# Softmax sums of an attention kernel: all key-tile additions on VectorE, first copies on GpSimd

## The chip, the cores and the metric

The kernel runs on one core of a Trainium2 chip. A core has a matrix engine (TensorE, shown as PE; its weight loads as PEld), a vector engine (VectorE, DVE), an activation engine (ScalarE, ACT), a general engine (GpSimd, POOL) and a sync engine (SyncE, SP) that here issues nearly all DMAs. They run side by side, each working through its own instructions in a fixed order, and meet at semaphores. The metric is the device time of one execution in microseconds; the median of the runs counts.

## What is computed

Two layers of a backbone over 256 context and 1,024 latent tokens, all in float32. Each layer has an input projection, four mixers side by side (a convolution, a gated linear attention called gla, a softmax attention, and a retention called ret), an output projection and an MLP. The part that matters is the softmax attention: 4 query heads share 2 key heads, 64 wide.

```python
def gqa_attend(q, k, v):
    s = jnp.einsum('bkgqd,bksd->bkgqs', q, k, preferred_element_type=jnp.float32) * ATT_DH ** -0.5
    p = jax.nn.softmax(s, axis=-1).astype(v.dtype)
    return jnp.einsum('bkgqs,bksd->bkgqd', p, v)
```

In layer 0 context and latent tokens are queries; in layer 1 only latent tokens are. Latent queries see all 1,280 keys, context queries only the 256 context keys.

## The kernel before

Tokens are cut into three tiles, t = 0 (256 context tokens), 1 and 2 (512 latent tokens each). Keys are taken 128 at a time: 10 key tiles for a latent token tile, 2 for the context tile.

`attention(g, side)` serves one key head g and its two query heads h_ = 0 and 1. It returns three generators: `prep` loads and transposes q and k, `rowmaxes` finds each query's largest score (matmuls into the PSUM tiles mb and pb, a maximum on VectorE, L972, and a few very small operations, L976 to L979), and `main(t)` does the softmax itself with keys on the partitions and queries along the columns. Its loop over key tiles, L1001 to L1022, is a pipeline one step deep. In step s, for each head: two matmuls write the scores of key tile s into an sb bank (L1006, L1007; two banks in all), and ScalarE takes the exponential into an SBUF tile aP (L1009; each head has its own aP with two buffers). For key tile s-1, for each head: a matmul of the values with aP adds to the output bank ob (L1014; the trace shows two PE instructions for each, since the data is float32), and the exponentials are added element by element to a running sum `sm[h_]`, a 128x512 tile that the trace calls acc (L1015 to L1021). The first key tile is copied into the sum instead (L1019). After the loop, matmuls with ones sum over the partitions (L1025), ScalarE forms the reciprocal with Ln and Exp (tile arc, L1027 and L1028), and VectorE multiplies into the result y (L1029).

Who does the copy and the additions is chosen by head: head 0 goes to GpSimd, head 1 to VectorE.

```python
eng = (nc.gpsimd, nc.vector)[h_]
if j == 0:
    eng.tensor_copy(sm[h_][:, :n], p_[:, :n])
else:
    eng.tensor_tensor(sm[h_][:, :n], sm[h_][:, :n], p_[:, :n], op=ALU.add)
```

An aP buffer can be written again when both its matmul and its addition are done, two steps later.

Attention is interleaved with the other mixers: `attend()` is stepped inside two loops, `pass1` (gla1 and ret1) and `pass2` (gla2 and ret2), and then drained. pass2 has GpSimd work of its own: L841 and L916 build the tiles gqe and rqe for small matmuls. After the drain the output projection loads its weights (wst), splits each into a rounded part on ScalarE (L159, whi) and a rest on VectorE (L160, wlo), splits y in the same way (ahi, alo), and starts the matmuls into `bank`.

The order in which each engine gets its instructions isn't the order of the code. A scheduler in the compiler orders them by their data, the free buffers, their place in the code and modelled durations, over all engines at once. So the weight splits of the output projection are found among the last steps of attention, and the two heads of a key tile do not always follow each other. A matmul helper `mm` has L166, a transpose helper `tr` L163, the activation helper `act` L153, so these lines appear for many stages; the tiles tell them apart.

Of the kernel before, what the change touches and what calls it, by code (L numbers as in the profile page):

```python
# [12 lines left out]
ALU = mybir.AluOpType  # L13
# [80 lines left out]
def build(tc, a, out, dbg=None):  # L94
    cst = a["cst"]
    nc = tc.nc
# [14 lines left out]
    def bank(tag="bank"):  # L111
        pool, bufs = P[tag]
        return pool.tile([128, 512], F32, tag=tag, name=tag, bufs=bufs)
# [104 lines left out]
    def open_w(slabs=5, stages=3):  # L218
        W["p"] = pools.get("wp", side="right", bufs=slabs)
        W["st"] = stages  # L220
# [136 lines left out]
            nc.vector.scalar_tensor_tensor(lo[:, k, :], s[:, :n], sh, hi[:, k, :].bitcast(F32),  # L357
                                           op0=ALU.add, op1=ALU.subtract)

    # ------------------------------------------------------------------ start  # L360
    open_w()
    open_act()
    xt = [xy_tile(t, "x") for t in range(3)]
# [50 lines left out]
    for l in range(2):  # L414
        last = l == 1
        tts = [1, 2] if last else [0, 1, 2]

        # -------------------------------------------------------- in projections
        def colA(sl, c0, t):
            b = bank()  # L420
            n = TOK[t][1]
            hi, lo = h[t]
            mm3(b[:, :n], [(sl[k // 2][0][:, k % 2, c0:c0 + 128], sl[k // 2][1][:, k % 2, c0:c0 + 128], hi[:, k, :], lo[:, k, :])
                           for k in range(KD)])
            return b
# [64 lines left out]
        for t in tts:  # L490
            o, n = TOK[t]
# [15 lines left out]
        for t in tts:  # L507
            o, n = TOK[t]
# [7 lines left out]

        pools.close("sg")

        # attention operands: rms norm and rotation, token-major
        aa = pools.get("aa", bufs=2)  # L520
        cosa = aa.tile([128, 8, 32], F32, name="cosa", bufs=1)
        sina = aa.tile([128, 8, 32], F32, name="sina", bufs=1)
# [64 lines left out]
        if l == 0:  # L587
            drain(small)

        # gated linear attention operands: decays, decayed queries and keys  # L590
        ag = pools.get("ag", bufs=2)
        tri = ag.tile([128, 512], F32, name="tri", bufs=1)
        ind = ag.tile([128, 2], F32, name="ind", bufs=1)
# [111 lines left out]
            emit_msc(0, 1)  # L705
        pools.close("ar", "convp", "actp", "wp", "psd")

        # -------------------------------------------------------- mixers
        open_psum("psa", sb=2, ob=1, mb=1, pb=1)
        open_psum("psm", gb0=1, gb1=1, rb=1)  # L710

# [218 lines left out]
        pass1 = both(stagger((gla1(i) for i in range(NTILE)), 3), stagger((ret1(i) for i in range(NTILE)), 3))  # L930
        pass2 = both(stagger((gla2(i) for i in back), 4), stagger((ret2(i) for i in back), 4))

        # -------------------------------------------------------- attention, one key head at a time
        at_ = pools.get("at", bufs=2)
        def attention(g, side):
            ap_ = pools.get(f"ap{g}", side=side, bufs=2)
            qa = ap_.tile([128, 2, NT], F32R, name="qa", bufs=1)
            ka = ap_.tile([128, NT], F32R, name="ka", bufs=1)
            kb = ap_.tile([66, NT], F32R, name="kb", bufs=1)
            mneg = ap_.tile([128, NTILE, 2, 2], F32R, name="mneg", bufs=1)  # L940
            ve = ap_.tile([128, NTILE, 64], F32, name="ve", bufs=1)
            nc.scalar.copy(kb[64:66, :], ones[0:2, 0:1].to_broadcast([2, NT]))

            def prep(i):
                need_q = not (last and i < CT)
                h0 = 0 if need_q else 2
                rw = at_.tile([128, 3, 64], F32, tag="arw", name="arw", bufs=4)
                nc.sync.dma_start(out=rw[:, h0:3, :], in_=attraw[i, :, g, h0 * 64:192].rearrange("p (h d) -> p h d", d=64))
                nc.sync.dma_start(out=ve[:, i, :], in_=attraw[i, :, g, 192:256])
                yield  # L950
                b = bank("pb")
                for j in range(h0, 3):
                    tr(b[0:64, j * 128:(j + 1) * 128], rw[:, j, :])
                cs = slice(i * 128, (i + 1) * 128)
                kp = b[0:64, 256:384]
                nc.scalar.copy(ka[0:64, cs], kp)
                nc.scalar.copy(ka[64:128, cs], kp)
                nc.vector.tensor_tensor(kb[0:64, cs], kp, ka[0:64, cs].bitcast(F32), op=ALU.subtract)
                if need_q:
                    qp = b[0:64, 0:256].rearrange("p (a b) -> p a b", a=2)  # L960
                    nc.scalar.copy(qa[0:64, :, cs], qp)
                    nc.vector.tensor_tensor(qa[64:128, :, cs], qp, qa[0:64, :, cs].bitcast(F32), op=ALU.subtract)

            def rowmax(i, h_):
                cs = slice(i * 128, (i + 1) * 128)
                kts = [(0, 256)] if i < CT else [(0, 512), (512, 512), (1024, 256)]
                mx = at_.tile([128, 4], F32, tag="amx", name="amx", bufs=4)
                for j, (ko, kn) in enumerate(kts):
                    b = bank(("mb", "pb")[(h_ + j) % 2])
                    mm(b[:, :kn], qa[:, h_, cs], ka[:, ko:ko + kn], True, False)  # L970
                    mm(b[:, :kn], qa[0:64, h_, cs], kb[0:64, ko:ko + kn], False, True)
                    nc.vector.reduce_max(mx[:, j:j + 1], b[:, :kn], axis=AX.X)  # L972
                    yield
                m = mx[:, 0:1]
                if len(kts) > 1:
                    nc.vector.reduce_max(mx[:, 3:4], mx[:, 0:3], axis=AX.X)  # L976
                    m = mx[:, 3:4]
                nc.vector.tensor_scalar(mneg[:, i, h_, 0:1], m, -1.0, None, op0=ALU.mult)
                nc.vector.scalar_tensor_tensor(mneg[:, i, h_, 1:2], m, -1.0, mneg[:, i, h_, 0:1].bitcast(F32),  # L979
                                               op0=ALU.mult, op1=ALU.subtract)  # L980

            def rowmaxes(t, h_):
                o, n = TOK[t]
                for j in range(n // 128):
                    yield from rowmax(o // 128 + j, h_)

            def main(t):
                o, n = TOK[t]
                qb = [ntmp(F32R) for h_ in range(2)]
                b = bank("sb")  # L990
                for h_ in range(2):
                    nc.scalar.copy(qb[h_][0:64, :n], qa[0:64, h_, o:o + n].bitcast(F32))
                    for j in range(n // 128):
                        mm(b[64 * h_:64 * h_ + 2, j * 128:(j + 1) * 128], mneg[:, o // 128 + j, h_, :].bitcast(F32), ident, True, True)
                    nc.scalar.copy(qb[h_][64:66, :n], b[64 * h_:64 * h_ + 2, :n])
                yield
                kts = list(range(CT if t == 0 else NTILE))
                bo = bank("ob")
                sm = [nacc() for h_ in range(2)]
                ps = {}  # L1000
                for step_ in range(len(kts) + 1):  # L1001
                    if step_ < len(kts):
                        js = slice(step_ * 128, (step_ + 1) * 128)
                        for h_ in range(2):
                            bs = bank("sb")
                            mm(bs[:, :n], ka[:, js], qa[:, h_, o:o + n], True, False)  # L1006
                            mm(bs[:, :n], kb[:, js], qb[h_][0:66, :n], False, True)  # L1007
                            p_ = at_.tile([128, 512], F32, tag=f"aP{h_}", name="aP")
                            act(p_[:, :n], bs[:, :n], AF.Exp, "exp", scale=0.125)  # L1009
                            ps[step_, h_] = p_  # L1010
                    if step_ > 0:
                        j = step_ - 1
                        for h_ in range(2):
                            mm(bo[64 * h_:64 * h_ + 64, :n], ve[:, j, :], ps[j, h_][:, :n], j == 0, j == kts[-1])  # L1014
                        for h_ in range(2):  # L1015
                            p_ = ps.pop((j, h_))
                            eng = (nc.gpsimd, nc.vector)[h_]
                            if j == 0:
                                eng.tensor_copy(sm[h_][:, :n], p_[:, :n])  # L1019
                            else:  # L1020
                                eng.tensor_tensor(sm[h_][:, :n], sm[h_][:, :n], p_[:, :n], op=ALU.add)  # L1021
                    yield  # L1022
                bs = bank("sb")
                for h_ in range(2):
                    mm(bs[64 * h_:64 * h_ + 64, :n], ones[:, 0:64], sm[h_][:, :n], True, True)  # L1025
                rc = at_.tile([128, 512], F32, tag="arc", name="arc", bufs=1)
                act(rc[:, :n], bs[:, :n], AF.Ln, "exp")  # L1027
                act(rc[:, :n], rc[:, :n], AF.Exp, "exp", scale=-1.0)  # L1028
                nc.vector.tensor_tensor(y[t][:, 4 + g, :], bo[:, :n], rc[:, :n], op=ALU.mult)  # L1029

            return prep, rowmaxes, main
# [53 lines left out]
        if "y" in dbg and dbg.get("l", 0) == l:  # L1085
            for t in tts:
                o, n = TOK[t]
                nc.sync.dma_start(out=dbg["y"][:, :, o:o + n], in_=y[t])

        # -------------------------------------------------------- out projection  # L1090
        open_dense()
        open_act()
        w_out = a["w_out"][l].rearrange("(k p) n -> p k n", p=128)
# [2 lines left out]
        for dh in range(2):  # L1096
            sl = [load_slab(w_out[:, 2 * q:2 * q + 2, dh * 512:(dh + 1) * 512], 2, 512) for q in range(4)]
            for t in tts:
                o, n = TOK[t]
# [18 lines left out]
                    h2[t] = act_tile(t)  # L1118
                    norm_mod(l, 1, xt[t], t, h2[t], acc[t])

        # -------------------------------------------------------- mlp
        w_up = a["w_up"][l].rearrange("(k p) n -> p k n", p=128)
        w_dn = a["w_down"][l].rearrange("(f p) n -> p f n", p=128)
        NF = FC // 128
# [83 lines left out]
        if "x" in dbg and dbg.get("l", 0) == l:  # L1208
            for t in tts:
                o, n = TOK[t]  # L1210
# [36 lines left out]
```

## Time and profile before

| what | before |
| --- | --- |
| runs | 3320.23, 3351.21, 3358.03 us |
| median | 3351.21 us |
| span of the profiled execution | 3332.9 us |
| PE, DVE, ACT, POOL busy | 97%, 53%, 28%, 7% of the span |

The span goes from the first to the last instruction of one profiled execution. The page gives no time for that execution beyond its span. The span is 18.3 us below the median of the runs and 12.7 us above the fastest of them. The attention loop with its sums occupies two stretches of it, about 570 to 795 us in layer 0 and 2305 to 2499 us in layer 1. A stage is read from its own stretch: which engine is busy there, who waits for whom, and how long one instruction of a kind takes.

### The profile page before, as it was taken

The page shows a single profiled execution, that of the slowest core. Times are in us where ns is not written, and L with a number is a line of the kernel's source. Part 1 is how long each engine was busy: PE and PEld are TensorE (multiplying, and loading weights), DVE is VectorE, ACT ScalarE, POOL GpSimd, SP SyncE. Part 2 cuts the span into 40 slices and gives each one's busy share as a digit, 9 for nine tenths or more (in the row PEclk, how much of TensorE's full clock was granted, in tenths as well). Part 3 has the DMA queues.
Part 4 walks back from the last instruction along what each step waited for, and adds up shares of the span by engine and source line. Part 5 has one row for each costly group of instructions (what it writes and reads, how often), then busy time and mean ns, then how long its engine had stood idle before and what let it go on. Part 6 is the DMA issues. An engine that isn't in the chain of part 4 may idle for free. (4 is left out here: it accounts for less than half of the span.)

```text
span 3332.9 us, 42190 instructions
## 1 busy us (share of the span) xinstructions
PE 3248.3 (97%) x17209; PEld 2475.9 (74%) x17209; DVE 1762.8 (53%) x3026; ACT 920.1 (28%) x1839; POOL 245.8 (7%) x255
## 2 busy tenths in 40 slices
PE   7999989999999999999999999899999999999999
PEld 5778856556888888888888779666557788888887
DVE  4683344676554444454446892235674644444545
ACT  4123432334322111111113334322243311111222
POOL 0011110331000000000000020201340000000000
PEclk8999997999999999999999999858899999999999
DMA  8354131003122222211111222210003111111111
GB/s 277 94 161 133 62 109 35 14 17 117 37 91 83 89 83 76 89 51 39 39 38 59 87 82 79 73 60 29 4 29 120 57 40 43 51 51 51 51 38 51
DMA packets 206523, 232.26 MB, mean 70 GB/s; under 512 B 19714, under 2 KB 160728, under 8 KB 206328
## 3 DMA queue, kind: packets, MB, share of 16 engines
q1 hardware_dynamic: 205592, 227.84, 21.4%
q8 instruction: 135, 2.21, 0.3%
q0 software_dynamic: 736, 1.72, 0.2%
q14 instruction: 60, 0.49, 0.0%
HBM read 191.11 MB, written 38.40 MB: 69 GB/s over the span
## 5 line engine op out<-in xcount | busy, mean ns | idle before, releaser
L166 PE MATMUL bank<-ahi,whi 128*128 128x512 f32 (+1 forms) x1920 | 720.0, 375 | 13.5 <-ACT tmp L153 6.6
L166 PE MATMUL bank<-ahi,wlo 128*128 128x512 f32 (+1 forms) x1920 | 720.5, 375 | 0.0
L166 PE MATMUL bank<-alo,whi 128*128 128x512 f32 (+1 forms) x1920 | 719.6, 375 | 0.9 <-DVE alo L357 0.9
L1156 DVE SCALAR_TENSOR_TENSOR x<-bank,mods,x 128x512 f32<-128x512 f32 (+1 forms) x640 | 438.5, 694 | 260.7 <-PE bank L166 259.0
L166 PE MATMUL bank<-hh,whi 128*128 128x512 f32 (+1 forms) x1280 | 475.9, 372 | 0.0
L166 PE MATMUL bank<-hl,whi 128*128 128x512 f32 (+1 forms) x1280 | 475.3, 371 | 0.0
L166 PE MATMUL bank<-hh,wlo 128*128 128x512 f32 (+1 forms) x1280 | 473.9, 370 | 0.0
L166 PEld LDWEIGHTS bank<-ahi,whi 128*128 128x128 f32 x1920 | 364.8, 190 | 100.5 <-DVE x L1156 8.2
L166 PEld LDWEIGHTS bank<-alo,whi 128*128 128x128 f32 x1920 | 362.9, 189 | 73.3 <-DVE alo L357 2.0
L166 PEld LDWEIGHTS bank<-ahi,wlo 128*128 128x128 f32 x1920 | 362.2, 189 | 67.8 <-issue 2.1
L160 DVE TENSOR_TENSOR wlo<-wst,whi 128x1024 fp32r<-128x1024 f32 (+1 forms) x186 | 224.9, 1223 | 269.1 <-ACT whi L159 268.9
L159 ACT CAST whi<-wst 128x1024 fp32r<-128x1024 f32 (+1 forms) x186 | 191.6, 1044 | 621.6 <-PE bank L166 473.1
L166 PEld LDWEIGHTS bank<-hh,whi 128*128 128x128 f32 x1280 | 240.5, 188 | 45.6
L166 PEld LDWEIGHTS bank<-hh,wlo 128*128 128x128 f32 x1280 | 239.9, 187 | 46.5 <-issue 0.2
L166 PEld LDWEIGHTS bank<-hl,whi 128*128 128x128 f32 x1280 | 240.4, 188 | 43.9 <-issue 0.2
L1140 ACT ACTIVATE tmp<-bank 128x512 f32<-128x512 f32 (+1 forms) x160 | 88.4, 553 | 658.5 <-PE bank L166 657.4
L1142 DVE TENSOR_TENSOR tmp<-tmp 128x512 f32<-128x512 f32 (+1 forms) x160 | 102.0, 639 | 308.5 <-ACT hh L1141 306.7
L166 PE MATMUL bank<-whi,ahi 128*128 128x512 f32 (+3 forms) x640 | 220.1, 346 | 8.3 <-ACT whi L159 8.3
L166 PE MATMUL bank<-wlo,ahi 128*128 128x512 f32 (+3 forms) x640 | 219.9, 344 | 4.2 <-DVE wlo L160 4.2
L166 PE MATMUL bank<-whi,alo 128*128 128x512 f32 (+3 forms) x640 | 216.6, 339 | 0.0
L463 DVE SCALAR_TENSOR_TENSOR yacc<-u,wdw,yacc 128x1295 f32<-128x1295 f32 (+1 forms) x120 | 166.4, 1432 | 0.3
L166 PEld LDWEIGHTS bank<-whi,ahi 128*128 128x128 f32 x640 | 122.0, 191 | 30.1 <-issue 9.2
(240 smaller groups left out, 3731.2 us busy)
## 6 DMA issues: line engine op xcount, KB each, us to landing
wm<-in_w_mod_dram SPq DMA_DIRECT2D x96, 512.0 KB, 4.1
wst<-in_w_up_dram SPq DMA_DIRECT2D x64, 512.0 KB, 4.2
wst<-in_w_down_dram SPq DMA_DIRECT2D x64, 512.0 KB, 3.5
wst<-in_w_in_dram SPq DMA_DIRECT2D x32, 512.0 KB, 4.6
graw<-glaraw SPq DMA_DIRECT2D x18, 512.0 KB, 3.4
wst<-in_w_out_dram SPq DMA_DIRECT2D x16, 512.0 KB, 4.0
x<-xdram SPq DMA_DIRECT2D x4, 2048.0 KB
glaraw<-gpre SPq DMA_DIRECT2D x18, 384.0 KB, 2.3
```

The lines of the kernel that those rows point to most:

```text
L159: nc.scalar.copy(hi, src)
L160: nc.vector.tensor_tensor(lo, src, hi.bitcast(F32), op=ALU.subtract)
L166: nc.tensor.matmul(ps, lhsT=lhsT, rhs=rhs, start=start, stop=stop)
L463: nc.vector.scalar_tensor_tensor(yv, uv, wv, yv, op0=ALU.mult, op1=ALU.add)
L1140: nc.scalar.activation(rl[:, :n], b[:, :n], AF.Relu)
L1142: nc.vector.tensor_tensor(rl[:, :n], rl[:, :n], rl[:, :n], op=ALU.mult)
L1156: nc.vector.scalar_tensor_tensor(xt[t][:, d, :], b[:, :n], mod(l, 5, d, seg), xt[t][:, d, :], op0=ALU.mult, op1=ALU.add)
```

## The change

The choice of the engine goes from the head to the kind of operation. Both heads' first copies are on GpSimd, and both heads' additions on VectorE. Eight comment lines become blank lines; they issue nothing. The core of the diff:

```diff
                         for h_ in range(2):
                             p_ = ps.pop((j, h_))
-                            eng = (nc.gpsimd, nc.vector)[h_]
                             if j == 0:
-                                eng.tensor_copy(sm[h_][:, :n], p_[:, :n])
+                                nc.gpsimd.tensor_copy(sm[h_][:, :n], p_[:, :n])
                             else:
-                                eng.tensor_tensor(sm[h_][:, :n], sm[h_][:, :n], p_[:, :n], op=ALU.add)
+                                nc.vector.tensor_tensor(sm[h_][:, :n], sm[h_][:, :n], p_[:, :n], op=ALU.add)
                     yield
```

## Rows read from the trace of the kernel before

**Rows 1.** The page, whole span: busy time, share and instructions of each engine.

```profile
PE 3248.3 (97%) x17209; PEld 2475.9 (74%) x17209; DVE 1762.8 (53%) x3026; ACT 920.1 (28%) x1839; POOL 245.8 (7%) x255
```

**Rows 2.** Windows of both attention stretches: busy us (instructions) by engine, then clock, DMA.

```profile
core 0: us, PE busy (x) PEld busy (x) DVE busy (x) ACT busy (x) POOL busy (x), PEclk, DMA share, GB/s
570.00:790.00 220.00, 218.01 (x1124) 115.95 (x1125) 149.41 (x353) 85.69 (x199) 73.11 (x60) 0.98 0.09 28
...
2305.00:2495.00 190.00, 190.00 (x926) 98.97 (x923) 129.99 (x294) 69.75 (x158) 67.17 (x56) 0.94 0.03 9
```

**Rows 3.** Waits, 565 to 800 us: engine, line waited for, total us, times, longest.

```profile
ACT aP L153 <- PE sb L166: 72.5, 46, 6.1
...
PEld sb L166 <- DVE acc L1021: 2.6, 2, 2.1
...
PEld sb L166 <- POOL acc L1021: 1.4, 2, 1.0
PE sb L166 <- DVE acc L1021: 1.2, 1, 1.2
```

**Rows 4.** Line L1021: count, ns min/median/max, forms. Then groups of VectorE by form (busy us, mean ns).

```profile
L1021 POOL TENSOR_TENSOR acc<-acc,aP x74: 724/1274/1964, 577.1 to 2496.8; 128x512 f32<-128x512 f32 x72, 128x256 f32<-128x256 f32 x2
L1021 DVE TENSOR_TENSOR acc<-acc,aP x74: 417/1441/1777, 577.4 to 2497.2; 128x512 f32<-128x512 f32 x72, 128x256 f32<-128x256 f32 x2
...
L1021 DVE TENSOR_TENSOR acc<-acc,aP 128x512 f32<-128x512 f32 x72 | 88.6, 1230 | 32.4 <-ACT aP L153 32.1
...
L757 DVE TENSOR_TENSOR fo<-fo,fss 128x256 f32<-128x256 f32 x36 | 19.8, 563 | 3.5 <-ACT fss L153 3.5
...
L1019 DVE COPY acc<-aP 128x512 f32<-128x512 f32 x8 | 3.3, 418 | 0.2 <-ACT aP L153 0.2
L1019 DVE COPY acc<-aP 128x256 f32<-128x256 f32 x2 | 1.1, 552 | 0.0
L1021 DVE TENSOR_TENSOR acc<-acc,aP 128x256 f32<-128x256 f32 x2 | 0.8, 421 | 0.1
```

**Rows 5.** Timeline, layer 0, heads in step: start us, us, engine, line, operation, count, idle before.

```profile
773.69 1.08 PE L166 MATMUL ob<-aP,ve 128*64 128x512 f32 x4
774.13 1.27 POOL L1021 TENSOR_TENSOR acc<-acc,aP 128x512 f32<-128x512 f32 x1 [0.88 <-ACT aP L153]
774.50 1.44 DVE L1021 TENSOR_TENSOR acc<-acc,aP 128x512 f32<-128x512 f32 x1 [0.71 <-ACT aP L153]
...
775.85 1.08 PE L166 MATMUL ob<-aP,ve 128*64 128x512 f32 x4
...
777.69 0.60 ACT L153 ACTIVATE aP<-sb 128x512 f32<-128x512 f32 x1
```

**Rows 6.** Timeline, layer 0, heads one at a time.

```profile
762.36 1.07 PE L166 MATMUL ob<-aP,ve 128*64 128x512 f32 x2
763.23 0.68 DVE L1021 TENSOR_TENSOR acc<-acc,aP 128x512 f32<-128x512 f32 x1
764.02 1.07 PE L166 MATMUL ob<-aP,ve 128*64 128x512 f32 x2
764.93 1.28 POOL L1021 TENSOR_TENSOR acc<-acc,aP 128x512 f32<-128x512 f32 x1 [1.71 <-ACT aP L153]
```

**Rows 7.** Timeline of PE: the first and the last such pair of ob matmuls.

```profile
573.69 1.07 PE L166 MATMUL ob<-aP,ve 128*64 128x512 f32 x2
...
2478.02 1.07 PE L166 MATMUL ob<-aP,ve 128*64 128x512 f32 x2
```

**Rows 8.** Timeline, layer 0, the end of the last 512-column tile.

```profile
782.74 1.58 POOL L1021 TENSOR_TENSOR acc<-acc,aP 128x512 f32<-128x512 f32 x1 [0.64 <-ACT aP L153]
783.10 1.76 DVE L1021 TENSOR_TENSOR acc<-acc,aP 128x512 f32<-128x512 f32 x1
...
784.79 1.21 DVE L160 TENSOR_TENSOR wlo<-wst,whi 128x1024 fp32r<-128x1024 f32 x1
785.92 0.68 DVE L1021 TENSOR_TENSOR acc<-acc,aP 128x512 f32<-128x512 f32 x1
...
786.66 1.07 PE L166 MATMUL sb<-acc,ones 128*64 128x512 f32 x2 [1.22 <-DVE acc L1021]
```

**Rows 9.** Timeline, layer 1, the last additions before the sums.

```profile
2496.82 1.27 POOL L1021 TENSOR_TENSOR acc<-acc,aP 128x512 f32<-128x512 f32 x1 [0.86 <-ACT aP L153]
2497.20 1.44 DVE L1021 TENSOR_TENSOR acc<-acc,aP 128x512 f32<-128x512 f32 x1 [0.69 <-ACT aP L153]
```

**Rows 10.** Windows, as group 2: two stretches of low clock inside attention.

```profile
621.00:634.00 13.00, 13.00 (x59) 8.16 (x57) 3.01 (x5) 1.93 (x4) 1.44 (x2) 0.61 0.01 1
...
2347.00:2372.00 25.00, 25.00 (x63) 11.49 (x62) 6.99 (x15) 5.38 (x10) 2.55 (x2) 0.53 0.00 0
```

**Rows 11.** Timeline of POOL, layer 0: a first copy behind pass2's work.

```profile
707.92 1.04 POOL L841 TENSOR_TENSOR gqe<-gq,c_blk 128x512 f32<-128x512 f32 x1 [6.31 <-PE gb L166]
708.90 0.81 POOL L1019 COPY acc<-aP 128x512 f32<-128x512 f32 x1
```

## Prediction

> **What bounds the kernel now.** I read the page first, then the windows of the two stretches in which the changed lines run, then the waits there, then the timeline of single steps. The page says that PE is busy for 97% of the span and POOL for 7% [rows 1]. That is a mean over stages, so the windows decide: in attention PE is busy 218.0 of 220 us in layer 0 and 190.0 of 190 in layer 1, while DVE is at 149.4 and 130.0, that is 68% each, and POOL at 73.1 and 67.2 [rows 2]. The engine whose work changes is not the one that is full.
>
> The waits say the same from the other side. ScalarE, which writes the exponentials, waits 72.5 us for the score matmuls (PE sb). In the same answer no row has it waiting for an addition to give back an aP buffer. PE itself stood idle once for an addition, for 1.2 us; the weight loads waited 2.6 us for VectorE's additions and 1.4 for GpSimd's [rows 3]. These few waits stand at the ends of tiles, where the matmuls with ones need the finished sums.
>
> A single step shows how much room the additions have. With the heads in step, the ob matmuls of two successive key tiles start at 773.69 and 775.85: a step takes 2.16 us of PE. The additions of one key tile start at 774.13 (POOL) and 774.50 (DVE) and end at 775.40 and 775.94. The buffer that the first of them read is written again at 777.69 [rows 5]. So an addition could come 2.3 us later (777.69 less 775.40), more than a whole step, before ScalarE noticed.
>
> **The price of an addition.** VectorE's 72 additions of 128x512 have a median of 1.44 us and a mean of 1.23 [rows 4], but one that meets no GpSimd addition takes 0.68 us [rows 6]. Where the two meet, VectorE's ends 0.54 us after GpSimd's: 775.94 against 775.40 [rows 5]. So the long ones are spent waiting for GpSimd, and the change takes that neighbour away. I price an addition after the change at 0.68 us (0.42 at 128x256); the upper end is 1.44. GpSimd's copies could hold additions up in the same way: 20 copies at no more than the 0.81 us of the one in [rows 11] are between 0 and 16 us.
>
> The Trainium skill gives a rule for this: "SBUF — State Buffer", section "Who interferes with whom", says that a VectorE instruction with two SBUF inputs and a GpSimd instruction that reads SBUF share a read interface, and that the later one is blocked until the other is done. The trace agrees, with 1.44 us beside GpSimd and 0.68 without. The rule speaks against the new place of the copies, which read SBUF too: by it the sum for VectorE tends to the upper of the two ends just given, and without it to the lower. The time of the kernel is the same by both as long as VectorE isn't full.
>
> **The change part by part.**
>
> *GpSimd loses 74 additions.* At a median of 1.27 us that is some 94 us of POOL [rows 4], off the path. It gains ten copies (two for each token tile and key head), 0.81 us at most by [rows 11]. Nothing shown waits for POOL in these stretches except the sums, so this part is worth nothing by itself.
>
> *VectorE gains 74 additions and loses ten copies.* After: 144 x 0.68 + 4 x 0.42 = 99.6 us. Before: 88.6 + 0.8 for its additions and 3.3 + 1.1 for its copies, 93.8 us [rows 4]. The difference is +5.8 us for twice the additions. Other VectorE work is stretched in the same way by GpSimd: the 36 multiplications of L757 took 563 ns on average, against 421 for an addition of the same width [rows 4], so up to 5.1 us go back. VectorE's load over both stretches, 279 us [rows 2], changes by +0.7 to +5.8 us (+22 with the copies at their worst), and goes from 68% to at most 74%. PE's 100% covers it. Without that cover, were VectorE the bound, this would cost these 0.7 to 22 us.
>
> *In one step.* Head 0's addition would run from 774.13 to 774.81 and head 1's from there to 775.49, before the 775.94 of today [rows 5]. The buffers come free earlier, which nobody waits for.
>
> *The ends of the tiles.* Here something is on the path. At the end of layer 1 the sums wait for the additions that end at 2498.09 and 2498.64 [rows 9]. One after the other on VectorE they would end at 2497.50 and 2498.18: 0.5 us earlier. At the end of layer 0's last wide tile the last addition ends at 786.60, since VectorE has weight splits of 1.21 us in between and an addition was held to 1.76 us; PE stood still for 1.22 us [rows 8]. Head 0's additions, 0.68 us each, take the place of such holds. Depending on where the splits fall, the last one ends about 1.2 us earlier or as late as now; I take 1.2, because the blocked time alone (1.76 less 0.68 for one addition) is nearly that much. The other tile ends are covered by interleaved matmuls.
>
> *New wait.* The addition of key tile 1 of head 1 now waits for a copy on GpSimd. That copy's queue also holds pass2's L841 and L916, and one L841 had waited 6.31 us for PE just before a copy [rows 11]. Behind the waiting addition on VectorE stand the row maxima, and for their banks PE waits. At the start of the ten tiles this is bounded by 0 and 10 x 6.31 = 63 us. I take 0: a copy normally has a whole step before its addition is due.
>
> *The order.* The compiler's scheduler orders all engines by modelled times, so PE's order may come out differently too. This is the largest unknown. PE is fast when the two heads' ob matmuls follow each other (four in 1.08 us) and slow when they come alone (two in 1.07): then half a step lasts 764.02 - 762.36 = 1.66 us, 3.32 for both heads instead of 2.16 [rows 5, 6]. Each half-step alone costs 0.58 us. Fifteen of the 160 wide half-steps are alone; the first and the last stand in [rows 7]. All of them in step would give 8.7 us; all 160 alone would cost 84. I take 0, since the additions have those 2.3 us of room and so need not move PE's order.
>
> **Sum.** 0.5 + 1.2 = 1.7 us less. The profiled span would go from 3332.9 to 3331.2 us. What lies around that span isn't given; the median of the runs is 18.3 us above it, and the runs lie 37.8 us apart. I put the sum on the median: 3351.2 - 1.7 = 3349.5 us. That can't be told from no change: about 1% (33.5 us) is what a measurement of this kernel can tell.
>
> **Rivals.**
>
> *Slower: the heads fall out of step.* Both heads' additions now queue on one engine, head 1's always last, behind row maxima and splits. If its buffer comes free late in the scheduler's model, PE's order alternates between heads. At 0.58 us each, 58 more half-steps alone make it 1% slower; with 80 it is 3396 us, with all 145 it is 3434. For it: this already happens at the start of tiles [rows 6, 7]. Against it: the 2.3 us of room.
>
> *Slower: VectorE waits behind GpSimd's copies,* as above. With three tiles of ten it is 3349.5 + 19 = 3368 us; it decides only from six tiles on.
>
> *An addition takes 1.44 us for itself.* Then two need 2.88 us in a step of 2.16, and VectorE bounds the steps where attention runs nearly alone. The timeline has 13 of them like the one in [rows 5]; at 0.72 us each that is 9.4 us: 3359. Against it: the 0.68 us of [rows 6].
>
> *Faster: order and clock fall well.* Inside attention the granted clock lay at 0.61 for 13 us and at 0.53 for 25 us [rows 10], that is mostly at 1.2 GHz instead of 2.4. If another order avoids both, 13 x 0.39 and 25 x 0.47 us are gone, 16.8 together, and with all heads in step 8.7 more: 3324 us. Nothing in the change aims at it. The same unknown can add a stretch.
>
> *VectorE is the bound in spite of PE's 100%.* The PEld share in the same windows is only 53% and 52% [rows 2]. Then VectorE's +0.7 to +5.8 us show directly: 3350 to 3355. The Trainium skill ("Perfetto Trace Analysis", section "Identifying the Most-Contended Engine") says that matmul busy time is a poor measure of headroom and weight-load busy time a better one. The trace does not bear out that VectorE is the bound: it idles for a third of the time, and PE hardly waits for it [rows 2, 3].
>
> **How the numbers follow.** The forecast, nothing that can be told apart, with VectorE as the bound included: 0.78; its own range is that of the runs, 3320 to 3358 less the 1.7, so 3318 to 3356. Out of step: 0.07. Behind the copies: 0.05. Additions of 1.44: 0.03. Order and clock: 0.07. Past 1%: faster takes half of the last case and 0.05 for the scatter of the runs, 0.09. Slower takes most of the first (0.05), a little of the second (0.02) and 0.05 for scatter, 0.12. Same: 0.79. The range goes from the fastest run less all heads in step, 3320.2 - 8.7 = 3311.5, to the slowest plus as many half-steps again alone and one more stretch of low clock like the longer one, 3358.0 + 8.7 + 11.8 = 3378.5.
>
> **What would show it.** Right: L1021 on DVE x148 with a median near 0.68 us; POOL with 20 copies and no addition; DVE's share near 70% and PE's near 100% in attention; ob matmuls in fours; the sums after layer 0's last wide tile about 1 us after the last exponential's matmul. Wrong: many ob matmuls in twos (out of step); DVE idle before L1021 with POOL as the releaser (behind the copies); L1021 still at 1.44 us; a stretch of low clock that is new or gone.

## The result, and the profile after

The changed kernel takes 3375.25 us (median of 18 runs, 3348.78 to 3398.15), the kernel before 3348.99 (18 runs, 3320.23 to 3377.95). The ratio is 1.0093, with a 95% interval of 1.0067 to 1.0118. (Ratios here compare fast runs alone, those within 1.5% of the fastest of their kernel, so a ratio can differ a little from that of two medians.) The forecast was no difference. The change makes the kernel a little slower: 0.9%, inside the range on record and short of 1%, but clearly apart from nothing.

In the profiled execution the span is 3380.6 us, where it was 3332.9. The page after, which answers to [rows 1], columns as there:

```profile
PE 3297.3 (98%) x17209; PEld 2497.6 (74%) x17209; DVE 1760.1 (52%) x3090; ACT 919.8 (27%) x1839; POOL 155.7 (5%) x191
```

GpSimd is 90 us less busy. VectorE has 64 instructions more and is not busier. In these two executions the time is in PE: 49 us more busy, with the same 17,209 instructions.

The additions themselves (view of the changed line L1020 and of the copies' line L1018, then VectorE's groups by form; they answer to [rows 4]):

```profile
L1020 DVE TENSOR_TENSOR acc<-acc,aP x148: 409/686/839, 606.2 to 2544.9; 128x512 f32<-128x512 f32 x144, 128x256 f32<-128x256 f32 x4
L1018 POOL COPY acc<-aP x20: 397/610/1172, 598.2 to 2521.5; 128x512 f32<-128x512 f32 x16, 128x256 f32<-128x256 f32 x4
...
L1020 DVE TENSOR_TENSOR acc<-acc,aP 128x512 f32<-128x512 f32 x144 | 95.3, 687 | 28.8 <-ACT aP L153 28.6
L757 DVE TENSOR_TENSOR fo<-fo,fss 128x256 f32<-128x256 f32 x36 | 19.0, 556 | 3.1 <-ACT fss L153 3.1
...
L1020 DVE TENSOR_TENSOR acc<-acc,aP 128x256 f32<-128x256 f32 x4 | 2.2, 570 | 0.0
```

An addition over 512 columns now takes 0.687 us on average. Before, VectorE's took 1.23, with a median of 1.44. No long ones are left: the longest takes 0.839. Of the 28.8 us that VectorE idled before these additions, 28.6 ended with ScalarE's exponentials, and none is put down to a copy on GpSimd.

The windows of both attention stretches after (columns as in [rows 2]):

```profile
597.00:822.00 225.00, 224.55 (x1071) 118.36 (x1070) 137.36 (x369) 76.04 (x182) 27.26 (x28) 0.91 0.06 18
2343.00:2543.00 200.00, 198.27 (x932) 99.89 (x932) 129.78 (x327) 70.14 (x161) 25.20 (x25) 0.94 0.03 9
```

PE is as full as before, and VectorE is at 61% and 65%. So the loss doesn't show as a wait: PE has the same matmuls to do and needs longer for them. Two things can do that, the order of the matmuls and the clock. The order first. A half-step is one head's part of a step, wide when it has 512 columns; it is alone when the ob matmuls of the other head don't stand beside its own. Timeline of PE in the changed kernel, layer 1, one piece with the heads one at a time and one with the heads in step:

```profile
2497.82 1.07 PE L166 MATMUL ob<-aP,ve 128*64 128x512 f32 x2
...
2498.82 0.50 PE L166 MATMUL sb<-qa,ka 128*128 128x512 f32 x1
2499.16 0.39 PE L166 MATMUL sb<-tmp,kb 66*128 66x512 f32 x1
2499.48 1.07 PE L166 MATMUL ob<-aP,ve 128*64 128x512 f32 x2
...
2541.85 1.08 PE L166 MATMUL ob<-aP,ve 128*64 128x512 f32 x4
...
2544.01 1.94 PE L166 MATMUL ob<-aP,ve 128*64 128x512 f32 x8
```

Alone, a half-step takes 2499.48 - 2497.82 = 1.66 us; a whole step in fours takes 2544.01 - 2541.85 = 2.16. Both are the values of [rows 5, 6]. The two heads write different halves of the ob bank, and four matmuls of both (1.08 us) take no longer than two of one head (1.07). What has changed is how many there are of each kind. In the program, 38 of the 160 wide half-steps are alone, where the kernel before has 16 (the prediction counted 15 in the trace). PE's order is the same until some way past the first ob matmul of layer 0, and 354 of its 15,029 matmuls and transposes stand at another place, all inside the attention stretches.

The clock. Windows of 150 us around both attentions (the last three columns are granted clock, DMA share, GB/s), first the kernel before:

```profile
450.00:600.00 150.00, 147.71 (x1155) 92.03 (x1155) 73.70 (x193) 42.02 (x144) 16.08 (x15) 0.89 0.19 56
600.00:750.00 150.00, 149.71 (x763) 82.29 (x761) 102.51 (x252) 53.82 (x132) 52.68 (x44) 0.97 0.05 13
2100.00:2250.00 150.00, 137.01 (x832) 91.25 (x830) 45.38 (x126) 37.35 (x114) 15.13 (x20) 0.67 0.23 71
2250.00:2400.00 150.00, 149.99 (x850) 84.76 (x850) 81.31 (x193) 39.94 (x102) 31.14 (x27) 0.86 0.05 17
```

and the changed kernel:

```profile
450.00:600.00 150.00, 148.44 (x952) 91.95 (x952) 56.08 (x152) 33.44 (x121) 8.93 (x10) 0.66 0.16 47
600.00:750.00 150.00, 149.69 (x775) 84.77 (x774) 89.23 (x236) 47.58 (x118) 21.28 (x22) 0.87 0.05 15
2100.00:2250.00 150.00, 135.59 (x858) 100.83 (x857) 49.56 (x124) 55.61 (x139) 19.23 (x25) 0.83 0.26 83
2250.00:2400.00 150.00, 149.99 (x936) 89.94 (x935) 69.08 (x187) 34.28 (x105) 11.00 (x12) 0.80 0.09 28
```

In the first window the changed execution has a clock of 0.66 against 0.89, that is more of the stretch at 1.2 GHz instead of 2.4. The first ob matmul comes at 600.92 us instead of 573.69, although PE's order up to there is the same. So some 27 of the 47.7 us between the two spans arose before any matmul stood at another place. Two single profiles can't show the effect of this change; it needs many runs, with each run's clock beside its time.

### The profile page after: what moved, and what is told of

It is laid out like the page before. It is cut to its first block, busy times and chain, and to the rows that moved or that the text cites. A ratio compares the mean times of both kernels' runs of the same rounds, so it can differ in the third digit from the quotient of the medians.

```text
span 3380.6 us, 42195 instructions
## 1 busy us (share of the span) xinstructions
PE 3297.3 (98%) x17209; PEld 2497.6 (74%) x17209; DVE 1760.1 (52%) x3090; ACT 919.8 (27%) x1839; POOL 155.7 (5%) x191
```

## How the experiments are read

Each run has its time and the mean granted clock of its core over the span. Over all runs that recorded both (235 runs of 14 kernels), one straight line for all kernels, with a level of its own for each kernel, leaves a scatter of 1.8 us. Its slope is 2.9 us for 0.001 of clock. From lowest to highest, the runs of one kernel lie 0.7 to 2.3% apart, almost only through their clock. The levels compare the kernels at the same mean clock, with 95% intervals of 1 to 2 us. The raw ratio stands beside them, because the clock that a kernel gets can be part of what it does.

"Alone" is the number of wide half-steps, of 160, that are left over when neighbouring ob matmuls of the two heads are paired off in the program's order; the groups of ob matmuls in each trace agree with it. One run of e9 at a mean clock of 0.663 (4320.68 us) is left out of the level.

| kernel | alone | ratio to before, 95% | mean clock | level against before, us |
| --- | --- | --- | --- | --- |
| before | 16 | 1 | 0.956 | 0 |
| after | 38 | 1.0093, 1.0067 to 1.0118 | 0.954 | +15.5 ± 0.9 |
| e1 after's engines, before's order | 16 | 1.0027, 0.999 to 1.0064 | 0.954 | +0.2 ± 1.1 |
| e2 before's engines, after's order | 38 | 1.0063, 1.0026 to 1.0101 | 0.954 | +15.6 ± 1.1 |
| e3 after's engines, heads in step | 2 | 1.0003, 0.9966 to 1.004 | 0.955 | -6.3 ± 1.1 |
| e4 before's engines, heads in step | 2 | 0.998, 0.9945 to 1.0016 | 0.956 | -9.9 ± 1.1 |
| e5 additions moved alone | 34 | 1.0049, 1.0016 to 1.0081 | 0.955 | +13.1 ± 1.1 |
| e6 copies moved alone | 14 | 0.9998, 0.9964 to 1.0031 | 0.957 | -0.2 ± 1.1 |
| e7 additions half as wide | 14 | 0.9976, 0.9941 to 1.0011 | 0.957 | -5.0 ± 1.1 |
| e8 before's engines, heads alternate | 136 | 1.024, 1.0199 to 1.0281 | 0.955 | +72.5 ± 1.5 |
| e9 after, third aP buffer | 34 | 0.9944, 0.9913 to 0.9976 | 0.961 | +9.6 ± 1.3 |
| e11 the same again | 34 | 0.9968, 0.993 to 1.0006 | 0.963 | +8.8 ± 1.2 |
| e10 before, maxima twice | 78 | 1.0222, 1.0189 to 1.0255 | 0.948 | +67.7 ± 1.6 |
| e12 e10 with before's order | 16 | 1.022, 1.0163 to 1.0276 | 0.944 | +35.7 ± 1.6 |

The question to them: is it the moved work on the engines, or the order in which TensorE gets its matmuls? And if the order, what moved it?

## Experiments 1 and 2: engines and order apart

In e1 the changed kernel gets TensorE's order from the kernel before, in e2 the kernel before gets the order of the changed one. Matmuls and transposes are noted down as they are issued, and before the program is ordered, each is tied to the one before it in a given list, without a semaphore. The list covers the attention stretches of both layers.

```diff
-        nc.tensor.matmul(ps, lhsT=lhsT, rhs=rhs, start=start, stop=stop)
+        return seen(nc.tensor.matmul(ps, lhsT=lhsT, rhs=rhs, start=start, stop=stop))
...
-    pools.close("psd", "dram", "xy01", "xy2", "nrm", "cpool")
+    force(tc, PEI, PE_ORDER); pools.close("psd", "dram", "xy01", "xy2", "nrm", "cpool")
...
+def force(tc, pei, orders):
+    for seq in orders:
+        for x, y_ in zip(seq, seq[1:]):
+            tc.add_manual_dep(pei[f"I-{y_}"], f"I-{x}", mybir.DependencyInfo(mybir.DependencyClass.NoSync,
+                              mybir.DependencyReason.DATA), reason="order")
```

> The changed kernel (all additions on VectorE, all first copies on GpSimd), but TensorE gets its matmuls of both attention stretches in exactly the order of the kernel before: 16 wide half-steps alone in place of 38. Theory A, the order: the 0.9% is the price of TensorE's order alone, so this is as fast as the kernel before, ratio 1.000 (0.997 to 1.003). Rival B, the engines: VectorE carries twice the additions and holds up TensorE, whatever the order, so the ratio stays at 1.009. Rival C, half and half: 22 half-steps alone at 0.58 us are 12.8 us, 0.4%; the other 0.5% comes from lower clock or from waits and stays, ratio 1.005.

> The kernel before (head 0 on GpSimd, head 1 on VectorE), but TensorE gets its matmuls of both attention stretches in exactly the order of the changed kernel: 38 wide half-steps alone in place of 16. Theory A, the order: as slow as the changed kernel, ratio 1.009. Rival B, the engines: 1.000. Rival C: 1.004, the 12.8 us of the half-steps without what the engines or the clock add.

Measured: e1 3356.12 us, e2 3372.12, beside 3355.86 for the kernel before. At the same clock e1 is at +0.2 us and e2 at +15.6, and the changed kernel is at +15.5. Whoever has the new order has the loss, and whoever has the new engines under the old order has none. By the raw ratios alone the two intervals overlap; it is the level at equal clock that separates them. VectorE's additions by form, first e1, then e2:

```profile
L1020 DVE TENSOR_TENSOR acc<-acc,aP 128x512 f32<-128x512 f32 x144 | 95.3, 687 | 28.5 <-ACT aP L153 25.3 <-ACT fss L153 2.9
```

```profile
L1021 DVE TENSOR_TENSOR acc<-acc,aP 128x512 f32<-128x512 f32 x72 | 86.8, 1205 | 36.8 <-ACT aP L153 36.4
```

e1 has the short additions of the changed kernel without its loss; e2 has the long ones of the kernel before (1205 ns on average) and the loss. PE in e2, with a GpSimd addition between two half-steps alone:

```profile
2485.56 1.07 PE L166 MATMUL ob<-aP,ve 128*64 128x512 f32 x2
2486.47 1.28 POOL L1021 TENSOR_TENSOR acc<-acc,aP 128x512 f32<-128x512 f32 x1 [3.11 <-ACT aP L153]
...
2487.22 1.07 PE L166 MATMUL ob<-aP,ve 128*64 128x512 f32 x2
```

It is the 1.66 us of the changed kernel, with the old engines.

## Experiments 3, 4 and 8: what one half-step alone costs

The same way of holding the order, with other lists: in e3 (engines of the changed kernel) and e4 (of the kernel before) the ob matmuls of both heads stand side by side; in e8, on the engines of the kernel before, head 0's are moved ahead of head 1's score matmuls. Each list is made from its own kernel's order, so e3 and e4 differ in the rest of the order too. In outline:

```diff
-PE_ORDER = [...]   # e1, e2: the order of the other kernel
+PE_ORDER = [...]   # e3, e4: ob of head 0, ob of head 1, with nothing between
+PE_ORDER = [...]   # e8: scores head 0, ob head 0, scores head 1, ob head 1
```

> The changed kernel, with TensorE's order in attention set so that the two heads' value matmuls always follow each other (2 wide half-steps alone in place of 38). Theory A: the 36 half-steps at 0.58 us give 21 us against the changed kernel's 3375, and the rest of its loss goes with the order too: 3341 us, ratio 0.997 to the kernel before. Rival B: the engines' loss stays and only the half-steps that the kernel before also had can be won: ratio 1.005 to 1.009. Rival C: 3354 us, ratio 1.0025.

> The kernel before with the same rule for TensorE's order: 2 wide half-steps alone in place of 16. By 0.58 us for each, 14 of them are 8.1 us less: ratio 0.9976, under all theories. If it is 1.000, a half-step alone costs less than the timeline says; if e3 and this one agree, where the additions run doesn't matter by itself.

> The kernel before with TensorE's order in attention set so that the heads alternate: 136 wide half-steps alone in place of 16. If a half-step alone costs the 0.58 us of the timeline, 120 more are 69.6 us: about 3425 us, ratio 1.021. If TensorE had slack that absorbs it, or if the 15.6 us of the changed order had another reason than the half-steps alone, less than half of that: ratio under 1.010.

Measured: 3350.81, 3342.95 and 3429.18 us. PE in e8, two half-steps after each other:

```profile
2577.41 1.07 PE L166 MATMUL ob<-aP,ve 128*64 128x512 f32 x2
...
2579.07 1.07 PE L166 MATMUL ob<-aP,ve 128*64 128x512 f32 x2
...
2580.73 1.07 PE L166 MATMUL ob<-aP,ve 128*64 128x512 f32 x2
```

The price follows from the differences of the levels:

| compared | half-steps alone | us at equal clock | us for each |
| --- | --- | --- | --- |
| e8 against before | 120 more | 72.5 | 0.60 |
| after against e3 | 36 more | 15.5 + 6.3 = 21.8 | 0.61 |
| before against e4 | 14 more | 9.9 | 0.71 |
| after against before | 22 more | 15.5 | 0.70 |
| e5 against before | 18 more | 13.1 | 0.73 |

The timeline had given 0.58. From 2 to 136 half-steps alone the loss goes with their number, in these comparisons at 0.60 to 0.73 us, and with either choice of engines. The number isn't everything: e3 and e4 have 2 each and lie 3.6 us apart, and e7, below, lies 4.8 us under e6 with the same 14.

## Experiments 5, 6 and 7: what moved the order

e5 moves the additions alone, e6 the copies alone.

```diff
 e5
-                                eng.tensor_tensor(sm[h_][:, :n], sm[h_][:, :n], p_[:, :n], op=ALU.add)
+                                nc.vector.tensor_tensor(sm[h_][:, :n], sm[h_][:, :n], p_[:, :n], op=ALU.add)
 e6
-                                eng.tensor_copy(sm[h_][:, :n], p_[:, :n])
+                                nc.gpsimd.tensor_copy(sm[h_][:, :n], p_[:, :n])
```

e7 is the changed kernel with additions over half the columns. It leaves out half of the sums and puts a fill with ones where the first copies were.

```diff
-                                nc.gpsimd.tensor_copy(sm[h_][:, :n], p_[:, :n])
+                                nc.gpsimd.memset(sm[h_][:, :n], 1.0)
-                                nc.vector.tensor_tensor(sm[h_][:, :n], sm[h_][:, :n], p_[:, :n], op=ALU.add)
+                                nc.vector.tensor_tensor(sm[h_][:, :n // 2], sm[h_][:, :n // 2], p_[:, :n // 2], op=ALU.add)
```

> One half of the change alone: all additions on VectorE, the copies by head as before. The order that the scheduler makes of it has 34 wide half-steps alone (the kernel before 16, the changed one 38). Theory: the additions bring the loss by way of the order, so 18 more at 0.58 us are 10.4 us more at equal clock, ratio 1.003 to 1.004. Rival: the loss comes with the copies, which now wait in GpSimd's queue; then 0 here, ratio 1.000.

> The other half alone: both first copies on GpSimd, the additions by head as before. The order has 14 wide half-steps alone. Theory: 1.2 us less than before at equal clock, ratio 0.9996. Rival (VectorE's second addition waits behind the copies): 5 to 15 us more, ratio 1.002 to 1.004.

> The changed kernel with all additions on VectorE, each over half of the columns only (the other half of the sums is left out, and the first copies are replaced by setting the sums to 1, so the softmax's sums are wrong). VectorE's work of additions is as in the kernel before, and the scheduler's order has 14 wide half-steps alone. Theory: what takes the heads apart is VectorE's load in the scheduler's reckoning, so the loss is gone: -1.2 us at equal clock, ratio 0.9996. Rival: that the two heads queue on one engine is enough by itself: 38 alone were to be seen, and a ratio of 1.005.

Measured: 3370.82, 3349.31 and 3342.65 us, beside 3356.5. The additions bring the loss (+13.1), the copies nothing (-0.2), and with half the width in each addition the loss is gone, though all of them are still on VectorE. So it isn't the choice of engine as such that takes the heads apart; how much the additions there have to do matters. e7 is 5.0 us below the kernel before, of which its two half-steps fewer alone account for about 1.4. Where the other 3.6 come from wasn't looked into.

## Experiments 9 and 11: a third aP buffer

The prediction's rival had a mechanism of its own: head 1's buffer comes free late in the compiler's reckoning. A third buffer for each head takes that away.

```diff
-                            p_ = at_.tile([128, 512], F32, tag=f"aP{h_}", name="aP")
+                            p_ = at_.tile([128, 512], F32, tag=f"aP{h_}", name="aP", bufs=3)
```

> The changed kernel with three instead of two aP buffers for each head; nothing else is edited, and the compiler orders it anew. Its program has 34 wide half-steps alone, against 38 of the changed kernel and 16 of the kernel before. Theory A (the order moved because VectorE's reckoned load rose, the buffers have no part in it): at the granted clock of the kernel before it is 18 x 0.60 to 0.73 = 11 to 13 us slower than that kernel, ratio about 1.0035 if the clock falls alike. Theory B (the heads fell out of step because a buffer comes free late in the compiler's reckoning, the mechanism that the prediction named for this rival): a third buffer takes the lateness away, and it is within 2 us of the kernel before at the same clock, ratio 1.000.

> The kernel of e9 once more, beside other runs of the kernel before. In e9 its mean granted clock was 0.961 against 0.953 of the kernel before, which made it faster by median although at the same clock it was slower by 9.6 us. Theory A (the clock of a run is scatter, not a property of the program): the clock is within 0.003 of that of the kernel before in this call, and the time is 8 to 13 us above that kernel, ratio 1.002 to 1.004. Theory B (this order of TensorE's work draws fewer stretches of low clock): the clock is again 0.006 to 0.010 higher and the ratio again 0.993 to 0.997.

Measured: 3349.68 us beside 3362.68, and in the repetition 3337.24 beside 3347.14. 34 half-steps stay alone, and at equal clock both are slower than the kernel before, by 9.6 and 8.8 us. That is 0.53 and 0.49 us for each of 18 more, a little under the other prices. A third buffer takes back 4 of the 22, so a late buffer is not what moved most of the order. Nor does the chip show one in the changed kernel's own trace: ScalarE waited once in both layers, in layer 1, for an addition to give a buffer back.

```profile
ACT aP L153 <- DVE acc L1020: 0.2, 1, 0.2
```

The raw ratios say the opposite, 0.9944 and 0.9968, because these runs had a higher clock: 0.961 against 0.953 for the kernel before in the same series, and 0.963 against 0.958 in the other. e11 was to tell whether that was scatter. The difference came again, smaller (0.0047, with a standard error of 0.0022) than expected if it belonged to the program and larger than expected of scatter. It stays open whether a third buffer is worth anything.

## Experiments 10 and 12: VectorE loaded by other work

In e10 the additions stay as before, and each row maximum is taken twice. e12 is the same kernel, held to TensorE's order in the kernel before.

```diff
                     nc.vector.reduce_max(mx[:, j:j + 1], b[:, :kn], axis=AX.X)
+                    nc.vector.reduce_max(mx[:, j:j + 1], b[:, :kn], axis=AX.X)
```

> The kernel before, its additions and copies untouched, but each maximum of L972 is taken twice, which puts work on VectorE that has nothing to do with the additions. Its program has 78 wide half-steps alone, 62 more than the kernel before. Theory A (VectorE's load, from whatever work, takes the heads apart, and each half-step alone costs 0.60 to 0.73 us): 37 to 45 us slower at the granted clock of the kernel before, ratio 1.011 to 1.0135, with no wait of TensorE for VectorE of that size in the trace. Theory B (only what is done to the aP buffers and the sums can move the order in a way that costs): the doubled maxima hide under TensorE, within 5 us of the kernel before, ratio 1.000 to 1.0015. If VectorE itself became the bound, the loss would stand in the trace as waits of TensorE for the maxima or the additions.

> The kernel of e10 (each maximum of L972 taken twice), with TensorE's matmuls held to the order that they have in the kernel before; 16 wide half-steps alone instead of 78. e10 was slower by 67.7 us at the same clock, where the half-steps alone account for 37 to 45. Theory A (most of it is TensorE's order, the rest waits for a VectorE that is now late here and there): 20 to 31 us slower than the kernel before at the same clock, ratio 1.006 to 1.009. Theory B (VectorE's doubled work is the bound and the order only follows it): 55 us or more slower, ratio 1.016 or more. Theory C (the order is everything, and each half-step alone of e10 cost 1.1 us): within 5 us, ratio 1.000 to 1.0015.

Measured: 3444.82 us beside 3362.68, and 3414.79 beside 3347.14. In e10, 78 half-steps are alone: work on VectorE that has nothing to do with the sums takes the heads apart too. The price is less clean than expected. e10 is at +67.7 us, above the 37 to 45 of the half-steps, and e12 is at +35.7, above the upper 31 of the likelier theory and far below the 55 of the other. The doubled maxima cost something by themselves. Who waited for them, in e10 (us, times):

```profile
  PE pb L166: 5.6, 6
  PE mb L166: 3.6, 5
```

and in e12:

```profile
  PE mb L166: 7.2, 11
  PE pb L166: 6.9, 10
```

All waits of PE for VectorE in the two attention stretches, summed from the lists of waits (420 to 870 and 2130 to 2570 us), are 14.6 us in the kernel before, 26.5 in e10 and 35.8 in e12. So e12 shows 21 of its 35.7 us as direct waits. Between e10 and e12 lie 32.0 us for 62 half-steps alone, 0.52 each; with the 9.3 us that e10 waits less, it is 0.67. By the raw ratios (1.0222 and 1.022) the two kernels can't be told apart: e12 had the lowest clock of all, 0.944. Here the clock is not plain scatter, and e12's clock loss may be part of what the waits did. The order's share in e10 therefore rests on the comparison at equal clock alone.

## Why the prediction was wrong, step by step

**The price of an addition: right.** 0.687 us on average for 0.68 predicted; the 1.44 us vanished with GpSimd's additions. Summed, 95.3 us and 2.2 for the four narrow ones (0.57 each for 0.42), 97.5 where 99.6 were forecast. The Trainium skill's rule ("SBUF — State Buffer", section "Who interferes with whom") fits: with GpSimd's additions beside them VectorE's took 1205 ns in e2, without them 687 in e1. What it let one fear of the copies did not come, since no addition was longer than 0.839 us.

**VectorE's load: right in size, off in detail.** Its busy time went from 1762.8 to 1760.1 us, where +0.7 to +5.8 had been expected in the two stretches. Of the up to 5.1 us that were to come back at L757, 0.8 did (556 ns for 563); together with other VectorE work it makes up the 6.4 us between +3.7 and -2.7.

**The ends of the tiles: right at the two that were priced, and too small to matter.** At the end of layer 1 the last group of ob matmuls and the first reciprocal start at (kernel before)

```profile
2496.39 1.94 PE L166 MATMUL ob<-aP,ve 128*64 128x512 f32 x8
...
2500.36 0.59 ACT L153 ACTIVATE arc<-sb 128x512 f32<-128x512 f32 x1
```

and in the changed kernel that group, shown above, starts at 2544.01 and the reciprocal at

```profile
2547.49 0.59 ACT L153 ACTIVATE arc<-sb 128x512 f32<-128x512 f32 x1
```

That is 3.97 us and then 3.48, 0.49 less for 0.5 predicted. After layer 0's last wide tile PE no longer stands still for an addition. The weight load of the sums waited

```profile
831.71 0.13 PEld L166 LDWEIGHTS sb<-acc,ones 128*64 128x64 f32 x1 [0.43 <-DVE acc L1020]
```

where PE itself had waited 1.22 us [rows 8]. In the time these 1.7 us don't show: e1 is at +0.2 ± 1.1. The other tile ends had been put at nothing, as covered by interleaved matmuls. At one of them, in layer 1, PE now waits for an addition:

```profile
2512.63 1.68 PE L166 MATMUL sb<-acc,ones 128*64 128x512 f32 x4 [1.08 <-DVE acc L1020]
```

In e1 PE waits for no addition, so this 1.08 us goes with the new order.

**The new wait for the copies: right at 0.** The line view above has no idle time of VectorE ended by GpSimd, and e6 is at -0.2 us.

**VectorE as the bound: not so.** All waits of PE for VectorE in the two attention stretches are 12.4 us after and 14.6 before.

**The order: this step failed.** The prediction took 0, "since the additions have those 2.3 us of room and so need not move PE's order". The room was real: ScalarE never waited more than 0.2 us for an addition to give a buffer back, and e1 shows that the new engines run under the old order at no cost. But room on the chip says nothing of what the compiler does when it sets the order beforehand. It made 22 more half-steps alone. At the prediction's own 0.58 us that is 12.8 us; measured were 15.5, at 0.70 each. The rival "the heads fall out of step" was the right one, with nearly the right price. Its chance of 0.07 was too low, because the argument against it was taken from the wrong place. The mechanism it named, a buffer that comes free late, is not borne out by e9 and e11 for more than 4 of the 22. What the runs show instead: doing more on VectorE takes the heads apart (e5 with the additions, e10 with maxima), doing half as much there keeps them in step (e7). By which quantity the compiler decides wasn't measured.

**The rest of the difference.** The means of the 18 runs each are 25.1 us apart. The order accounts for 15.5. The changed kernel's mean clock, 0.9543 (standard error 0.0011), lies 0.0013 below that of all 94 recorded runs of the kernel before, 3.7 us at 2.9 us for 0.001; the remaining 6 us are that the first 18 runs of the kernel before, which have no clock on record, were faster on average than those 94. Whether the lower clock belongs to the change or is scatter can't be told at this size. So the order is shown to cost 15.5 us, about 0.5%, and not the whole 0.9%.

**The range, and what can be told apart.** The median lies inside the range partly by luck: its upper end had room for 15 more half-steps alone (8.7 us) and one more stretch of low clock (11.8 us), and the order alone took 15.5. The prediction also took 1% for the least that a measurement of this kernel can tell; 18 runs of each give the ratio to 0.25%, and the comparison at equal clock gives 1 to 2 us.

**What follows for the kernel.** Under the orders of the kernel before and of the changed one the moved additions cost nothing that can be told (e1, e2), and the order is what costs. With the heads held in step, the engines of the kernel before are 9.9 us better than that kernel at equal clock (e4), and e3, with the engines of the changed one, is 6.3 better. Whether the 3.6 us between e4 and e3 come from the engines or from the rest of the order, in which the two differ, no run here shows. By the raw ratio e4 (0.998, 0.9945 to 1.0016) can't be told from the kernel before.

## What to carry to other kernels

Where a compiler orders the instructions, work moved between two engines that have room can reorder a third one that has none. Before costing such a move at nothing, count in the program's order the pattern that the full engine is fast in, before and after, and price the difference from the timeline. Where a kernel's runs differ by more than the effect sought, compare them at equal clock, and do not read the cause from two single profiles.

## What the hardware showed that was not expected

**Time against clock.** Of one and the same program, runs lie 0.7 to 2.3% apart, and nearly all of it goes with the mean granted clock at 2.9 us for 0.001, with a scatter of 1.8 us left. In the windows above, around the two attentions, the clock goes from 0.66 to 0.97. From 450 to 600 us it is once 0.89 and once 0.66; the order of the matmuls is the same there, save that the kernel before gets further in it and is in the attention from 573.69 on.

**The clock isn't the same for all programs.** e12 ran at 0.944 with the kernel before at 0.958 in the same series; e9 and e11 ran 0.005 to 0.008 above the kernel before of their series. PE idled more in e12, waiting 35.8 us for VectorE in those stretches instead of 14.6. What drew the clock up in e9 and e11, no run here shows.
